# A streaming-encoder layer on one core: the order of side work in three late stages changed

## The chip, the cores and the metric

The kernel runs on one core of a Trainium2 chip. The metric is the device time of one execution, in microseconds (us). Three executions of the kernel before took 1586.19, 1580.94 and 1584.56 us; the median is 1584.56.

TensorE (PE, with PEld for its weight loads) multiplies matrices into PSUM, VectorE (DVE), ScalarE (ACT) and GpSimd (POOL) work elementwise, and SyncE (SP) issues nearly all transfers between the chip's memory and SBUF. Each engine runs its own instructions in order and waits for others by semaphores.

## The reference

One layer on x of 1024 frames by 1024 channels, all in 32-bit floats:

```python
for li in range(DEPTH):                                  # DEPTH = 1
    h = rmsnorm(x, norm_mix_g[li])
    z = h @ w_in[li]
    qa, fa, ia, ga, qb, kb, vb, gate_a, gate_b = jnp.split(z, split_at, axis=-1)
    oa = hgrn2_mixer(qa, fa, ia, ga, lower_bounds[li], hgrn_onorm_g[li])
    ob = band_attention(qb, kb, vb, ...)
    merged = (jax.nn.sigmoid(gate_a) * (oa @ w_branch_a[li])
              + jax.nn.sigmoid(gate_b) * (ob @ w_branch_b[li]))
    x = x + merged @ w_out[li]
    h2 = rmsnorm(x, norm_ffn_g[li])
    x = x + (jax.nn.silu(h2 @ w_ffn_gate[li]) * (h2 @ w_ffn_up[li])) @ w_ffn_down[li]
    h3 = rmsnorm(x, norm_ple_g[li])
    x = x + jax.nn.sigmoid(h3 @ w_ple_gate[li]) * (p[li] @ w_ple_proj[li])
return x
```

The feed-forward width is 2816, p has 256 columns.

## The kernel before, in words

**Layout.** The layer's x lies as eight tiles of 128 channels by 1024 frames. A matmul multiplies 128x128 weights by 128x512 operands into one PSUM bank of 128x512 (`pm`). To keep 32-bit accuracy, every operand is split into a high part, rounded by a cast on ScalarE, and a low rest, subtracted on VectorE or GpSimd; one product of two operands is three matmuls (`gemm`).

**Stages, in order of time.** The token mixers; 16 gate tiles, of which four are computed plainly and twelve in six Strassen units of two; the two branch products with their gates (`branches`, eight weight tiles); the output projection; the feed-forward gate and up products (22 Strassen units); the product down; and the last stage, `ple`, which computes the last line of the loop and stores the result.

**Products of seven passes.** The output projection, down and the last stage use the Strassen-Winograd scheme on 2x2 blocks: `passes` (L976) runs seven passes in the order of `KINDS` (L973): A11, S2, A12, S3, S1, A22, S4, each a weight block against an operand block B11, T2, B21, T3, T1, T4, B22. Three groups of four banks, x, y and z, accumulate chains of passes (`CHAIN`). In the last stage a pass has four steps (k) of four banks, 48 matmuls, and after a pass `after` (L1748) works on each of its four banks (u = 0 to 3). Its results are P1 (A11's), u2 and u3; `V.tensor_tensor(ps, ps, u2[u], ALU.add)` behind S1 adds u2 = P1+P6 into the banks of chain z, on which S4 then goes on. S4 runs bank by bank, the last bank in two halves of 256 frames (`last`, L1768).

**Finishing a tile of the last stage** (`out`, L1729) is a generator of four pieces: scaling by the rms row on VectorE (in place), a sigmoid on ScalarE, the product with the embedding e on VectorE (e<-t,e), and the addition of x, by GpSimd if nothing else is given, with the store issued by SP behind it (L1741). `todo` holds the tiles under way; `some(4)` moves four of them one piece on.

**Work beside the matmuls.** Each stage has a generator `side` of which one piece is issued after each step of the products; it holds sums for operands, loads, splits (`m_split`, L949: a cast on ScalarE and a subtraction s<-s,s of 128x1024 on VectorE) and the norm's rows. So the place of a `yield` sets where in an engine's order a piece stands.

**The order on the engines.** The instructions of V, A, G (VectorE, ScalarE, GpSimd through `Pinned`, L53), of TensorE (L82, L85) and of `load` and `store` (SP, L77) are chained by hand in the order in which the program issues them. The store in `out` is a plain `nc.sync.dma_start` outside that chain, which the scheduler places.

**Weights.** `weights` (L127) keeps a ring of four split tiles (`RING`) over two raw tiles (`RAW`): SP loads the raw tile (wr), ScalarE casts it (wh, L122), GpSimd subtracts the rest (wl, L125). `ahead` says how many tiles are prepared before they are used. In the Strassen units `strassen_weights` (L1389) makes sums of the next unit's weights on VectorE (q), casts them (whi) and takes the rest (wlo); `strassen_load` fetches the unit after that.

**Accumulating transfers.** Sums of weight blocks for the output projection and for down are made in the chip's memory: `dma_sums` (L1057) first copies blocks by SP and then adds others by DMAs that GpSimd issues (d<-in_wq and d<-d). Gate units, branches and feed-forward units take the additions one by one from the queue `self.adds` with `next(self.adds, None)` (L857, L909, L926, L1539); in a gate unit with every second piece of `side`, in a branch with each weight tile.

**Operands of the last stage.** `m_order` lists the operand tiles, two for each pass; `m_split` takes the next and puts it into `m_ready`, from which `operand` (L1778) takes. The first four splits are issued in down's last two passes (`down_side`, L1602), the rest in the last stage itself.

## Time and profile before

| what | us |
|---|---|
| three executions, median | 1584.56 |
| the profiled execution | 1583.47 |
| its span, from the first to the last instruction | 1581.7 |
| TensorE busy, of a mean granted clock of 0.997 | 1553.5 |
| busy in the span's last stretch, 1490 to 1582: TensorE | 79.99 |
| VectorE there | 62.99 |
| ScalarE there | 42.28 |
| GpSimd there | 42.75 |

The stretches by stage, with TensorE's (PE), its weight loads' (PEld), VectorE's, ScalarE's and GpSimd's busy time, each with its count of instructions, then the granted clock, the busy share of the DMA engines and their GB/s:

```profile
0.00:330.00 330.00, 320.60 (x2174) 285.28 (x2174) 195.10 (x384) 88.80 (x143) 93.56 (x53) 1.00 0.19 66
330.00:640.00 310.00, 306.96 (x1944) 261.30 (x1944) 236.67 (x597) 189.87 (x441) 79.64 (x49) 1.00 0.49 142
640.00:700.00 60.00, 58.63 (x255) 47.40 (x254) 27.92 (x30) 18.14 (x23) 22.34 (x14) 1.00 0.95 307
700.00:882.00 182.00, 181.69 (x815) 150.21 (x815) 147.67 (x156) 88.36 (x116) 69.32 (x36) 1.00 0.55 177
882.00:1252.00 370.00, 367.87 (x1616) 304.11 (x1615) 281.62 (x309) 104.64 (x156) 218.87 (x129) 1.00 0.38 114
1252.00:1490.00 238.00, 237.75 (x1050) 196.53 (x1049) 154.28 (x137) 106.64 (x125) 121.04 (x52) 1.00 0.67 244
```

Mixers and attention fill the first two rows and more; the branches begin at about 666 us, the feed-forward's first up unit runs near 886, down from about 1252 and the last stage from about 1490.

A row of the profile reads: start in us, duration, engine, line, operation, tile out<-in, size; in square brackets the time that the engine stood idle before, and whose work ended it. The span of a row on GpSimd is rough. A matmul row may stand for several.

### The profile page before, as it was taken

What the parts mean: (1) busy time and instruction counts of PE and PEld (TensorE: products, weight loads), DVE (VectorE), ACT (ScalarE), POOL (GpSimd) and SP (SyncE); (2) the same over time, 40 slices, a digit from 0 to 9 for tenths busy, and PEclk for the clock granted to TensorE, in tenths of its full rate; (3) what the DMA queues carried; (4) which work ended last, traced back from release to release, by engine and by line L of the source; (5) the groups of instructions that cost most, each with busy time, mean ns of one, the idle gap of its engine ahead of it and who ended that gap; (6) DMA issues with size and microseconds to landing.
All of it is one profiled execution on the core that took longest, in us unless ns stands there. A gap on an engine that the chain in (4) does not pass through costs nothing.

```text
span 1581.7 us, 21492 instructions
## 1 busy us (share of the span) xinstructions
PE 1553.5 (98%) x8224; PEld 1311.6 (83%) x8224; DVE 1106.2 (70%) x1685; ACT 638.7 (40%) x1059; POOL 647.5 (41%) x353
## 2 busy tenths in 40 slices
PE   8999999999999999999999999999999999999997
PEld 6998988888888888788888788888888888888886
DVE  5656765378777876644898777777777757755577
ACT  5321221167677633321467322322222244455462
POOL 3422221223113044337320555666665545545453
PEclk9999999999999999999999999999999999999999
DMA  5101100362433466897344334444433288775334
GB/s 189 54 28 41 41 28 28 105 196 80 141 114 127 153 153 174 225 320 239 107 157 171 132 113 127 132 129 127 121 117 109 85 303 323 278 275 180 124 110 173
DMA packets 83527, 230.38 MB, mean 146 GB/s; under 512 B 8928, under 2 KB 9568, under 8 KB 82912
## 3 DMA queue, kind: packets, MB, share of 16 engines
q1 hardware_dynamic: 76880, 213.26, 38.5%
q0 software_dynamic: 6400, 15.73, 6.2%
q8 instruction: 64, 1.05, 0.3%
q14 instruction: 39, 0.32, 0.1%
q10 hardware_dynamic: 144, 0.02, 0.0%
HBM read 179.43 MB, written 81.00 MB: 165 GB/s over the span
## 4 chain that ended last, share of the span: by engine, by line
PE 78%; DVE 9%; DMA 2%; POOL 2%; ACT 2%; issue 2%; SPq 0%; DVEq 0%; ACTq 0%; POOLq 0%
PE pm L82 76%; DVE s L53 6%; PE pm L85 3%; DVE m L53 1%; POOL wl L125 1%; DMA wr<-d 1%; ACT s L53 1%; DMA s<-d 1%; ACT wh L122 1%; POOL s L53 1%; DVE q L53 0%; DVE t L53 0%; DMA wr<-in_ba 0%; DMA wr<-in_dw 0%; DVE wl L125 0%
## 5 line engine op out<-in xcount | busy, mean ns | idle before, releaser
L82 PE MATMUL pm<-s,wh 128*128 128x512 f32 (+1 forms) x1712 | 532.7, 392 | 7.2 <-ACT wh L122 5.3
L82 PE MATMUL pm<-s,whi 128*128 128x512 f32 x1568 | 484.2, 390 | 2.4 <-DVE t L53 2.4
L125 POOL TENSOR_TENSOR wl<-wr,wh 128x1024 fp32r<-128x1024 f32 (+2 forms) x100 | 248.5, 2495 | 361.3 <-ACT wh L122 346.9
L82 PEld LDWEIGHTS pm<-s,wh 128*128 128x128 f32 x1712 | 319.8, 189 | 75.8 <-ACT wh L122 5.3
L82 PEld LDWEIGHTS pm<-s,whi 128*128 128x128 f32 x1568 | 294.8, 188 | 64.2 <-DVE t L53 3.2
L53 DVE TENSOR_TENSOR s<-s,s 128x512 f32<-128x512 f32 (+3 forms) x228 | 281.9, 1269 | 79.1 <-ACT s L53 41.5
L82 PE MATMUL pm<-s,wl 128*128 128x512 f32 (+1 forms) x856 | 333.8, 390 | 0.5 <-POOL wl L125 0.5
L82 PE MATMUL pm<-s,wlo 128*128 128x512 f32 x784 | 305.7, 390 | 0.0
L82 PE MATMUL pm<-wh,s 128*128 128x256 f32 (+1 forms) x896 | 237.6, 340 | 0.0
L122 ACT CAST wh<-wr 128x1024 fp32r<-128x1024 f32 (+2 forms) x114 | 115.0, 1010 | 277.3 <-PE pm L82 155.6
L82 PEld LDWEIGHTS pm<-s,wl 128*128 128x128 f32 x856 | 161.2, 188 | 34.3 <-POOL wl L125 1.4
L53 DVE TENSOR_TENSOR t<-pm,t 128x512 f32<-128x512 f32 x138 | 95.1, 689 | 126.1 <-PE pm L82 107.4
L82 PEld LDWEIGHTS pm<-s,wlo 128*128 128x128 f32 x784 | 147.6, 188 | 31.5 <-DVE wlo L53 0.6
L82 PEld LDWEIGHTS pm<-wh,s 128*128 128x128 f32 x896 | 154.4, 190 | 14.0
L53 POOL TENSOR_TENSOR wlo<-wr,whi 128x512 fp32r<-128x512 f32 (+1 forms) x53 | 113.7, 2154 | 91.7 <-PE pm L82 67.2
L82 PE MATMUL pm<-wl,s 128*128 128x256 f32 (+1 forms) x448 | 147.5, 329 | 0.8 <-POOL wl L125 0.8
L53 POOL TENSOR_TENSOR wlo<-q,whi 128x512 fp32r<-128x512 f32 x52 | 81.7, 1571 | 86.1 <-ACT whi L53 52.9
L53 ACT CAST s<-s 128x1024 fp32r<-128x1024 f32 (+1 forms) x94 | 90.1, 980 | 58.3 <-DVE s L53 34.7
L53 POOL TENSOR_TENSOR s<-t,rb 128x512 f32<-128x512 f32 x44 | 71.6, 1627 | 98.8 <-ACT t L53 98.8
L53 ACT CAST whi<-q 128x512 fp32r<-128x512 f32 (+1 forms) x81 | 61.4, 758 | 99.3 <-PE pm L82 94.6
L53 ACT ACTIVATE t<-s 128x512 f32<-128x512 f32 x44 | 27.8, 633 | 159.0 <-DVE s L53 155.0
L82 PEld LDWEIGHTS pm<-wl,s 128*128 128x128 f32 x448 | 85.4, 191 | 6.3 <-POOL wl L125 1.0
(144 smaller groups left out, 1798.9 us busy)
## 6 DMA issues: line engine op xcount, KB each, us to landing
s<-d SPq DMA_DIRECT2D x67, 512.0 KB, 5.9
d<-s SPq DMA_DIRECT2D x87, 256.0 KB, 2.3
wr<-d SPq DMA_DIRECT2D x36, 512.0 KB, 3.5
wr<-in_sg SPq DMA_DIRECT2D x22, 512.0 KB, 3.7
wr<-in_su SPq DMA_DIRECT2D x22, 512.0 KB, 4.1
s<-in_x SPq DMA_DIRECT2D x21, 512.0 KB, 7.8
d<-in_wq SPq DMA_DIRECT2D x20, 512.0 KB, 9.5
d<-s SPq DMA_DIRECT2D x18, 512.0 KB, 5.2
```

The source lines that it names most:

```text
L53: return lambda *a, **k: self.trunk.order(op(*a, **k), self.key)
L82: return self.order(self.nc.tensor.matmul(*a, **k))
L85: return self.order(self.nc.tensor.transpose(*a, **k))
L122: self.nc.scalar.copy(hi[:, c], raw[:, c])
L125: rest.tensor_tensor(lo[:, c], raw[:, c], f32(hi[:, c]), ALU.subtract)
```

## The change

Five things are changed, all in the order or the place of work; what is computed stays the same, and no matmul is added or removed.

1. The last two of the six gate units no longer take additions from `self.adds` (`n < units - 2`). Four accumulating DMAs less are issued there; the queue stays in order, so each later taker gets an addition four places earlier in the queue, and its last four are issued in the feed-forward units 18 to 21, which took none.
2. In the first up unit (n == 1) of `ff_pairs`, `side` yields once before it starts the sums of the next weights.
3. `warm`, a tile of one column, gets a silu in the second branch and a sigmoid before down's last pass, and nobody reads it.
4. B22's two splits move from the last stage into down's sixth pass (`m_early`).
5. In the last stage, S3's result is taken over with a subtraction of u2 on VectorE where ScalarE copied it. The addition of u2 into the banks of chain z moves from behind S1 into `side`, after two of S1's four steps; the accumulation group of a bank is closed there (`cut`). In `out`, x is added by VectorE for A12's tiles (GpSimd before), by GpSimd for S1's and S4's (VectorE before), except the last half bank's, which stays with VectorE; A22's stay with GpSimd. The store is chained into SP's order, and A12's come one piece later (`late`). `last` finishes all tiles under way before the last bank's.

```diff
...
@@ -853,7 +853,7 @@
                     self.strassen_load()
                 yield
                 for i, _ in enumerate(more):
-                    if i % 2:
+                    if i % 2 and n < units - 2:
                         next(self.adds, None)
                     yield
 
@@ -936,6 +936,8 @@
                     yield 2592
             if dd == 1:
                 self.branch_sums(0)
+            if dd == 1:
+                self.A.activation(self.warm, self.ones, AF.Silu)
             if dd == 2:
                 self.x, self.xd = [], [None] * KC
                 for c in range(KC):
@@ -973,8 +975,8 @@
     KINDS = (("A11", "B11"), ("S2", "T2"), ("A12", "B21"), ("S3", "T3"), ("S1", "T1"), ("A22", "T4"), ("S4", "B22"))
     CHAIN = {"A11": "x", "A12": "x", "S2": "y", "S3": "y", "A22": "y", "S1": "z", "S4": "z"}
 
-    def passes(self, npairs, operand, after, side, last=None):
-        banks = {}
+    def passes(self, npairs, operand, after, side, last=None, banks=None):
+        banks = {} if banks is None else banks
         for kind, b in self.KINDS:
             chain = self.CHAIN[kind]
             if last and kind == "S4":
@@ -1000,6 +1002,7 @@
             if fresh:
                 banks[chain] = [self.mm() for _ in range(4)]
             ps = banks[chain]
+            cut = 1 if last and kind == "S1" else npairs
             for k in range(npairs):
                 i, j = divmod(k, 2)
                 if j == 0:
@@ -1010,7 +1013,7 @@
                     c = slice(j * HALF + u * P, j * HALF + u * P + P)
                     drain(self.gemm(
                         ps[u], [(w[0][:, c], w[1][:, c], hi[:, s], lo[:, s])], first=fresh and k == 0,
-                        last=k == npairs - 1, **({} if fresh else {"skip_group_check": True})))
+                        last=k in (npairs - 1, cut), **({} if fresh and k <= cut else {"skip_group_check": True})))
                 next(side, None)
                 yield 0
             for u in range(4):
@@ -1528,6 +1531,8 @@
             def side():
                 more = self.strassen_weights() if n + 1 < units else self.down_first()
                 keep = self.keep_acts(n // 2 - 1) if n % 2 == 0 else iter(())
+                if n == 1:
+                    yield
                 next(more, None)
                 if n + 2 < units:
                     self.strassen_load()
@@ -1621,14 +1626,20 @@
                 self.ple_part("B22", (i - 35) // 2)
             yield
         drain(sums)
-        self.m_order = [(b, i) for _, b in self.KINDS for i in range(2)]
+        self.m_order = [("B22", i) for i in range(2)]
         self.m_ready = []
         for i in range(11):
             if i < 8 and i % 2 == 0:
                 self.ple_part("B11", i // 2)
-            if i in (4, 8):
+            if i in (1, 3):
                 self.m_split()
-            yield
+            if i == 3:
+                self.m_early, self.m_ready = self.m_ready, []
+                self.m_order = [(b, i) for _, b in self.KINDS[:6] for i in range(2)]
+            if i in (5, 8):
+                self.m_split()
+            yield
+        self.A.activation(self.warm, self.ones, AF.Sigmoid)
         for i in range(11):
             if i < 4:
                 self.ple_part("B12", i)
@@ -1716,7 +1727,7 @@
         nc, V, A, G = self.nc, self.V, self.A, self.G
         h0, h1 = slice(0, HALF), slice(HALF, T)
         p1, u2, u3 = [[t[:, h] for t in (self.slot(), self.slot()) for h in (h0, h1)] for _ in range(3)]
-        es = {}
+        es, banks = {}, {}
 
         def load(odd, h):
             tiles = [self.slot() for _ in range(2)]
@@ -1726,7 +1737,7 @@
 
         todo = []
 
-        def out(c, h, t, add=G, sp=None):
+        def out(c, h, t, add=V, sp=None, late=True):
 
             sp = sp or slice(0, HALF)
             t, e = t[:, sp], es[c, h.start][:, sp]
@@ -1738,7 +1749,9 @@
             V.tensor_tensor(e, t, e, ALU.mult)
             yield
             add.tensor_tensor(e, e, self.x[c][:, at], ALU.add)
-            nc.sync.dma_start(self.out[c][:, at], e)
+            if late:
+                yield
+            self.store(self.out[c][:, at], e)
 
         def some(n):
 
@@ -1755,20 +1768,21 @@
                 todo.append(out(2 * u, h1, ps))
                 next(todo[-1])
             elif kind == "S3":
-                A.copy(u3[u], ps)
+                V.tensor_tensor(u3[u], ps, u2[u], ALU.subtract)
             elif kind == "S1":
                 V.tensor_tensor(u3[u], ps, u3[u], ALU.add)
-                V.tensor_tensor(ps, ps, u2[u], ALU.add)
-                todo.append(out(2 * u + 1, h0, u3[u], V))
+                todo.append(out(2 * u + 1, h0, u3[u], G, late=False))
             elif kind == "A22":
-                todo.append(out(2 * u + 1, h1, ps))
+                todo.append(out(2 * u + 1, h1, ps, G, late=False))
                 next(todo[-1])
                 next(todo[-1])
 
         def last(u, ps, sp):
             for _ in range(max(0, min(2, len(todo) - u))):
                 drain(todo.pop(0))
-            stream = out(2 * u, h0, ps, V, sp)
+            while u == 3 and todo:
+                drain(todo.pop(0))
+            stream = out(2 * u, h0, ps, V if u == 3 and sp.start else G, sp, late=False)
             next(stream)
             next(stream)
             todo.append(stream)
@@ -1776,6 +1790,8 @@
                 drain(todo.pop(0))
 
         def operand(b, i):
+            if b == "B22":
+                return self.m_early.pop(0)
             got = self.m_ready.pop(0)
             if len(self.m_ready) < 2:
                 self.m_split()
@@ -1819,7 +1835,10 @@
             del todo[:]
 
             load(1, h1)
-            for i in range(4):
+            yield
+            for u, ps in enumerate(banks["z"]):
+                V.tensor_tensor(ps, ps, u2[u], ALU.add)
+            for i in range(3):
                 yield
             load(0, h0)
             for i in range(4):
@@ -1828,7 +1847,7 @@
                     del todo[:4]
                 yield
 
-        yield from self.passes(4, operand, after, side(), last)
+        yield from self.passes(4, operand, after, side(), last, banks)
         while todo:
             drain(todo.pop(0))
 
```

**GpSimd at the end of the gate units.** The rows are GpSimd's order from the last but one gate unit into the branches; wlo are rests of summed weights, wl of the branches' first weights (in_ba), d the sums in memory. Before:

```order
L53 TENSOR_TENSOR wlo_6529<-wr_6386,whi_6528 128x512
L53 DMA d_3462<-in_wq 256x1x512
L53 TENSOR_TENSOR wlo_6565<-wr_6388,whi_6564 128x1024
L53 TENSOR_TENSOR wlo_6588<-q_6546,whi_6587 128x512
L53 DMA d_3846<-in_wq 256x1x512
L53 TENSOR_TENSOR wlo_6647<-q_6627,whi_6646 128x512
L53 DMA d_3539<-in_wq 256x1x512
L125 TENSOR_TENSOR wl_6667<-wr_6669,wh_6668 128x1024
```

Changed:

```order
L53 TENSOR_TENSOR wlo_6529<-wr_6386,whi_6528 128x512
L53 TENSOR_TENSOR wlo_6565<-wr_6388,whi_6564 128x1024
L53 TENSOR_TENSOR wlo_6587<-q_6546,whi_6586 128x512
L53 TENSOR_TENSOR wlo_6645<-q_6625,whi_6644 128x512
L125 TENSOR_TENSOR wl_6665<-wr_6667,wh_6666 128x1024
L125 TENSOR_TENSOR wl_6671<-wr_6673,wh_6672 128x1024
L125 TENSOR_TENSOR wl_6677<-wr_6679,wh_6678 128x1024
L53 TENSOR_TENSOR wl_6821<-wr_6823,wh_6822 128x1024
```

The three additions d<-in_wq in this piece are gone from between the rests; the next one stands with the branches' later weights.

**VectorE at the first up unit.** The rows are VectorE's order at the seam; q are sums for the next unit's weights, t<-pm,t sums of a finished product's bank (pm) with an earlier one, s the gate tiles. Before:

```order
L53 TENSOR_TENSOR t_8490<-pm_8102,s_7985 128x512
L53 TENSOR_TENSOR s_8384<-t_8490,rb_8405 128x512
L53 TENSOR_TENSOR q_8521<-wr_8500,wr_8502 128x512
L53 TENSOR_TENSOR q_8521<-q_8521,wr_8500 128x512
L53 TENSOR_TENSOR t_8544<-pm_8505,t_8519 128x512
L53 TENSOR_TENSOR q_8546<-wr_8500 128x512
L53 TENSOR_TENSOR wlo_8549<-q_8521,whi_8548 128x1024
L53 TENSOR_TENSOR t_8579<-pm_8505,t_8519 128x512
```

Changed:

```order
L53 TENSOR_TENSOR t_8487<-pm_8099,s_7982 128x512
L53 TENSOR_TENSOR s_8381<-t_8487,rb_8402 128x512
L53 TENSOR_TENSOR t_8530<-pm_8502,t_8516 128x512
L53 TENSOR_TENSOR q_8532<-wr_8497,wr_8499 128x512
L53 TENSOR_TENSOR q_8532<-q_8532,wr_8497 128x512
L53 TENSOR_TENSOR q_8555<-wr_8497 128x512
L53 TENSOR_TENSOR t_8572<-pm_8502,t_8516 128x512
L53 TENSOR_TENSOR t_8572<-pm_8503,t_8572 128x512
L53 TENSOR_TENSOR s_8381<-t_8572,s_8381 128x512
L53 TENSOR_TENSOR wlo_8558<-q_8532,whi_8557 128x1024
```

The two q sums that stood ahead of t_8544<-pm_8505 stand behind the same sum, now t_8530<-pm_8502.

**SP and VectorE in the last stage.** The rows are SP's order from S1's last weights on; wr are raw weights (from d, the sums in memory, or in_gw), s<-d loads of e, out<-s the stores of A12's tiles. Before:

```order
L77 DMA wr_13494<-d_12457 128x1024
L77 DMA wr_13544<-in_gw 128x1024
L77 DMA wr_13598<-in_gw 128x1024
L1741 DMA out<-s_13348 128x512 x2
L1741 DMA out<-s_13349 128x512 x2
L77 DMA s_13614<-d_8072 128x512
L77 DMA s_13614<-d_8074 128x512
L77 DMA s_13615<-d_8076 128x512
L77 DMA s_13615<-d_8078 128x512
L77 DMA wr_13634<-d_12023 128x1024
```

Changed:

```order
L77 DMA wr_13504<-d_12458 128x1024
L77 DMA wr_13554<-in_gw 128x1024
L77 DMA out<-s_13358 128x512 x2
L77 DMA out<-s_13359 128x512 x2
L77 DMA wr_13604<-in_gw 128x1024
L77 DMA s_13620<-d_8069 128x512
L77 DMA s_13620<-d_8071 128x512
L77 DMA s_13621<-d_8073 128x512
L77 DMA s_13621<-d_8075 128x512
L77 DMA wr_13644<-d_12024 128x1024
```

The four stores (two rows of two) stand ahead of the third weight load in place of behind it.

**VectorE in the same place.** Rows of 128x1024 are splits; s_13204, s_13205 and s_13214, s_13215 are u3's tiles, s_13202, s_13203 and s_13212, s_13213 u2's; pm_13592 to pm_13595 and pm_13598 to pm_13601 are the banks of chain z, pm_13332 to pm_13335 those of S3. Before:

```order
L53 TENSOR_TENSOR s_13539<-s_12768,s_13538 128x1024
L53 TENSOR_TENSOR s_13569<-s_12847,s_13568 128x1024
L53 TENSOR_TENSOR s_13585<-s_12571,s_13584 128x1024
L53 TENSOR_TENSOR s_13204<-pm_13592,s_13204 128x512
L53 TENSOR_TENSOR pm_13592<-pm_13592,s_13202 128x512
L53 TENSOR_TENSOR s_13204<-pm_13593,s_13204 128x512
L53 TENSOR_TENSOR pm_13593<-pm_13593,s_13202 128x512
L53 TENSOR_TENSOR s_13205<-pm_13594,s_13205 128x512
L53 TENSOR_TENSOR pm_13594<-pm_13594,s_13203 128x512
L53 TENSOR_TENSOR s_13205<-pm_13595,s_13205 128x512
L53 TENSOR_TENSOR pm_13595<-pm_13595,s_13203 128x512
```

Changed:

```order
L53 TENSOR_TENSOR s_13575<-s_12856,s_13574 128x1024
L53 TENSOR_TENSOR s_13214<-pm_13332,s_13212 128x512
L53 TENSOR_TENSOR s_13214<-pm_13333,s_13212 128x512
L53 TENSOR_TENSOR s_13215<-pm_13334,s_13213 128x512
L53 TENSOR_TENSOR s_13215<-pm_13335,s_13213 128x512
L53 TENSOR_TENSOR pm_13598<-pm_13598,s_13212 128x512
L53 TENSOR_TENSOR pm_13599<-pm_13599,s_13212 128x512
L53 TENSOR_TENSOR pm_13600<-pm_13600,s_13213 128x512
L53 TENSOR_TENSOR pm_13601<-pm_13601,s_13213 128x512
L53 TENSOR_TENSOR s_13214<-pm_13598,s_13214 128x512
L53 TENSOR_TENSOR s_13214<-pm_13599,s_13214 128x512
```

Two of three splits are gone ahead of S1's results, the subtractions of S3's banks have come in, and the four additions into pm stand as a group ahead of those to u3, one by one behind each of them before.

4 lines of the change are left out of this document (2 added, 2 removed).

## The prediction

> **What bounds the kernel now.** I read the page's busy line first, then busy time by stretches, then the chain of waits.
>
> ```profile
> span 1581.7 us, 21492 instructions
> PE 1553.5 (98%) x8224; PEld 1311.6 (83%) x8224; DVE 1106.2 (70%) x1685; ACT 638.7 (40%) x1059; POOL 647.5 (41%) x353
> ...
> 1560.00:1571.00 11.00, 10.54 (x58) 9.02 (x56) 11.00 (x19) 2.91 (x5) 2.59 (x3) 1.00 0.29 111
> 1571.00:1582.00 11.00, 0.00 (x0) 0.00 (x0) 7.16 (x14) 1.90 (x4) 2.85 (x2) 0.71 0.46 175
> ```
>
> TensorE (first pair in a stretch) has work for 1553.5 of 1581.7 us, and no matmul is added or removed. What can be won is the 28.2 us in which it has none, and time at a lower clock. The biggest piece is the end: from 1571 on it does nothing, while VectorE (third pair) is full before that and still busy after. The chain of waits names the other places:
>
> ```profile
> 656.31 10.35 DMA s<-d
> 666.74 1.05 ACT s L191
> 667.82 1.24 DVE s L192
> 669.10 85.08 PE pm L82 x374
> ...
> 886.12 366.39 PE pm L82 x1608
> ...
> 1537.95 6.75 POOL s L53 x3
> 1547.07 6.36 DMA wr<-d
> ```
>
> The change touches three of its breaks: a load at the branch stage's start, VectorE at the seam of gate and up, and the last stage. I cost each.
>
> **Four additions moved.** These are accumulating DMAs issued by GpSimd; they leave the last two gate units for later stages.
>
> ```profile
> 656.20 1.07 POOL L53 DMA_DIRECT2D d<-in_wq  x1 [1.73 <-issue]
> ...
> q0 software_dynamic: 779, 1.50, 34.9%
> ...
> 660.00:670.00 10.00, 8.63 (x35) 5.99 (x34) 9.41 (x9) 5.13 (x7) 2.07 (x1) 1.00 1.05 312
> ...
> 666.12 0.40 PE L82 MATMUL pm<-s,wh 128*128 128x512 f32 x1
> 666.68 0.50 PE L82 MATMUL pm<-s,wh 128*128 128x512 f32 x1 [0.17 <-DVE s L192]
> ...
> 667.84 0.49 PE L82 MATMUL pm<-s,wh 128*128 128x512 f32 x1 [0.42 <-ACT s L191]
> 669.10 0.50 PE L82 MATMUL pm<-s,wh 128*128 128x512 f32 x1 [0.77 <-DVE s L192]
> ```
>
> Matmuls start 0.227 us apart where nothing is missing (85.08/374 in the chain). From 666.12 to 669.10 are four steps (one start, between the second and third row, is left out): 2.98 us where 0.91 would do, so 2.07 are lost. The last two rows wait for the fourth load, its cast and its remainder. That load took 10.35 us in a stretch whose DMA share is 1.05. The queue row is of 645 to 672: additions took 34.9% of 27 us for 1.50 MB, so one of 512 KB takes 3.1 us of all engines. Without the one issued at 656.20 the load lands near 663.6, its cast ends at 664.7 and its remainder at 665.9, before it is asked for. The first two steps lose a few tenths to other tiles, so I take 1.8; the bounds are 0 (the loads crowd each other) and 2.07. At their new places the four add 4x1.07 us to GpSimd and 3.1 us of DMA each to units where the chain shows TensorE unbroken for 366.39 us although most of them carry one already: nothing.
>
> **The seam.** In the first up unit the sums for later weights come one product later, so VectorE meets the sum that frees a bank (t<-pm,t) first.
>
> ```profile
> 882.00 1.78 DVE L53 TENSOR_TENSOR q<-wr,wr 128x512 f32<-128x512 f32 x1
> 883.82 1.64 DVE L53 TENSOR_TENSOR q<-q,wr 128x512 f32<-128x512 f32 x1
> 885.38 0.68 DVE L53 TENSOR_TENSOR t<-pm,t 128x512 f32<-128x512 f32 x1
> 885.98 1.16 DVE L53 TENSOR_TENSOR q<-wr 128x512 f32<-128x512 f32 x1
> ...
> 883.21 0.58 ACT L53 COPY t<-pm 128x512 f32<-128x512 f32 x1
> ...
> 883.60 0.39 PE L82 MATMUL pm<-s,wlo 128*128 128x512 f32 x1
> 886.12 1.13 PE L82 MATMUL pm<-s,whi 128*128 128x512 f32 x2 [2.13 <-DVE t L53]
> ...
> 889.61 0.42 PE L82 MATMUL pm<-s,wlo 128*128 128x512 f32 x1
> ...
> 886.00:890.00 4.00, 3.88 (x10) 3.07 (x11) 3.37 (x3) 1.48 (x2) 4.00 (x3) 0.57 0.00 0
> ```
>
> The sum needs ScalarE's copy, done at 883.79. With the two q sums behind it, it runs from 883.82 to 884.50 and TensorE goes on at 884.56 in place of 886.12: 1.56. The wait also cost speed: the granted clock behind it is 0.57, and the eight steps from 886.12 to 889.61 took 3.49 us where 8x0.227 is 1.82: 1.67. A wait of 0.7 is left; those of 0.42 and 0.77 above left the clock at 1.00. Together 3.2. [...] Late next: the q sums (1.78+1.64+1.16) end at 889.1, the next t (0.7) at 889.8, and the product that needs its bank starts two products of 12 steps later, 884.56+24x0.227=890.0. So the bounds are 0 (the wait comes back there, clock and all) and 4.0 (no wait left).
>
> Preloading the two activation tables removes a load from the way of a sigmoid and of a silu that both wait for VectorE longer: nothing.
>
> **The last stage.**
>
> ```profile
> 1522.71 3.41 DVE L53 TENSOR_TENSOR s<-s,s 128x1024 fp32r<-128x1024 f32 x1
> 1528.44 1.21 DVE L53 TENSOR_TENSOR s<-s,s 128x1024 fp32r<-128x1024 f32 x1
> 1533.58 2.47 DVE L53 TENSOR_TENSOR s<-pm,s 128x512 f32<-128x512 f32 x4
> 1558.72 6.61 DVE L53 TENSOR_TENSOR s<-s,s 128x1024 fp32r<-128x1024 f32 x9 [4.74 <-ACT s L53]
> 1565.26 2.48 DVE L53 TENSOR_TENSOR pm<-pm,rb 128x512 f32<-128x512 f32 x4
> 1578.34 0.43 DVE L53 TENSOR_TENSOR s<-s,s 128x256 f32<-128x256 f32 x1
> ...
> 1535.66 9.39 SPq L1741 DMA_DIRECT2D out<-s  x4
> ...
> 1553.53 2.12 ACT L122 CAST wh<-wr 128x1024 fp32r<-128x1024 f32 x2 [14.20 <-DMA wr<-d]
> ...
> 1554.66 4.78 POOL L125 TENSOR_TENSOR wl<-wr,wh 128x1024 fp32r<-128x1024 f32 x2 [7.62 <-ACT wh L122]
> 1568.41 5.44 POOL L53 TENSOR_TENSOR s<-s,s 128x512 f32<-128x512 f32 x4 [8.97 <-DVE s L53]
> ...
> 1543.03 0.61 PE L82 MATMUL pm<-s,wh 128*128 128x512 f32 x2
> 1570.27 0.28 PE L82 MATMUL pm<-s,wl 128*128 128x256 f32 x1
> ...
> wr<-d SPq DMA_DIRECT2D x36, 512.0 KB, 3.5
> ```
>
> Now: four stores hold SP from 1535.66, since each waits for a GpSimd addition (2.25 each by the chain's row); the last weights load at 1547.07, ScalarE stands 14.20 us for them, and VectorE goes on only at 1558.72, with a split of B22 and eight more ahead of A22's results. It reaches those at 1565.26 and is 8.2 us behind when TensorE ends at 1570.55; from its end (1578.77) to the span's are 2.92.
>
> Then: x for A12 is added by VectorE, two splits of 1.2 to 3.4 are gone, ten of its later additions go to GpSimd, and the last loads leave SP near 1542. It gains four subtractions (ScalarE's copies before), and its four additions P1+P6 now stand in the middle of S1, where TensorE waits for them. What that costs: the e products end at 1536.05 now (1533.58+2.47), and 2.2 earlier, 1533.9, if the split ahead of them takes 1.21 in place of 3.41 (ScalarE now casts T1 ahead of the weights). Behind them stand two splits (1.21 each), four x additions, four subtractions (2.48/4=0.62 each) and the first addition (0.7): 8.1. A split beside GpSimd takes up to 2.2 more. TensorE asks at 1543.03; the addition is ready from 1542.0 to 1546.4, so the wait is 0 to 3.4. I take the early start and one split held 1.9, 1543.9: a wait of 0.8. The other three follow at 0.68, TensorE's own pace. Behind the waiting matmul stand S1's second half, A22 and S4, so the wait goes to the end in full.
>
> Then the load of A22's second weights is behind the A12 stores, not ahead. It would leave SP near 1540 and is needed in mid A22, 1554; load, cast and remainder are 3.5+1.06+2.4 (the page's row on landing, 2.12/2, 4.78/2), so they end by 1547. No cost.
>
> At the end: S1 ends 24 steps behind its middle, 1543.9+5.4=1549.3, the additions to u3 0.7 later; scaling and e products take 8x0.62=5.0, held by one remainder (2.4) and some of GpSimd's additions: 1559 at the latest; A22's eight steps of 0.62 end by 1564; S4's first quarter comes 60 steps behind S1, 1562.9. So VectorE is within a step when TensorE ends at 1571.35. Behind that stand scaling, ScalarE's sigmoid, product and addition of the last half quarter, at 0.43 each, and 0.3 that I allow for the gaps between the engines: 1573.4, and with 2.92 the span ends at 1576.3: 5.4 gained. Bounds: 6.2 without the mid-pass wait; 1.5 with that wait at its longest plus 1.7 for the clock.
>
> **Sum:** 1.8+3.2+5.4=10.4. The profiled execution took 1583.47, so 1573.1; it is 1.1 under the median, 1584.56, from which it is 1574.2. I forecast 1573.5.
>
> **Rivals.**
> - *The seam's wait moves to the fifth product.* For it: 0.2 us to spare, and q sums stretched to 1.78 beside GpSimd. 3.2 lost: 1576.7. Chance 0.12.
> - *VectorE is late in mid S1.* For it: 3.41 for a split of 1.21. Against: only two remainders of GpSimd lie there. 3.4+1.7 in place of 0.8: 1577.8. Chance 0.12.
> - [...] Chance 0.05.
> - *The loads crowd each other, and both waits above come too:* 1582.8, no change. Chance 0.09.
> - *GpSimd becomes the bound* of the last stage. Twelve additions at 2.25 (6.75/3 in the chain, the pace beside VectorE) behind the last remainder, at 1559.4 as before, end at 1586.4; with 2.9 and the wait of 0.8 the span is 1590.1, less 5.0 from the other places 1585.1, 3.4 more than now: 1586.9 to 1588.0 by the two bases, 1587.4, slower. It decides from about 2.0 us for each. Against: 5.44 for four, 1.36 each, once VectorE works on PSUM. [...] Chance 0.06.
>
> The forecast keeps 0.56. A measurement of this kernel can tell about 0.3% (4.75 us) from no change, so faster means under 1579.8. Forecast and the first three rivals lie there, 0.85; a little goes for their spread: faster 0.83, within 0.1, slower 0.07. The range: 1573.5 less 1.6 (the three upper bounds) and 2.6 (half the spread of the runs), 1569.5; above, the second rival plus 2.6, 1580.5.
>
> **What would show it.** TensorE without breaks near 667 and a clock of 1.00 behind the seam; a break under 1 us in mid S1; ScalarE's 14.20 for wr<-d gone; at most 5 us from the last matmul to the last VectorE row and store. A clock under 1.00 after 1540, or a GpSimd row as the last one before the final store, would prove it wrong.

## The result, and the profile after

| | before | changed |
|---|---|---|
| median of six runs, us | 1583.92 | 1573.98 |
| lowest to highest | 1580.94 to 1586.19 | 1573.47 to 1576.64 |
| profiled execution | 1583.47 | 1574.29 |
| its span | 1581.7 | 1572.5 |
| from TensorE's last matmul to the span's end | 11.15 | 5.99 |

The ratio, taken over all runs, is 0.9942, with a 95% interval of 0.9929 to 0.9955: faster by 9.2 us of 1583.9, between 7.1 and 11.2 (the two medians alone lie 9.9 apart). The forecast was 1573.5.

The page of the changed kernel's profile, its span and busy times:

```profile
span 1572.5 us, 21502 instructions
PE 1551.8 (99%) x8224; PEld 1311.9 (83%) x8224; DVE 1108.8 (71%) x1685; ACT 636.2 (40%) x1057; POOL 646.9 (41%) x357
```

As many matmuls as before in 9.2 us less. The chain of waits of the changed kernel, its late links (start, duration, engine, tile):

```profile
858.22 633.04 PE pm L82 x2796
1491.80 33.47 PE pm L82 x159
1526.43 11.74 DVE s L53 x14
1538.92 27.61 PE pm L82 x132
```

The links over a load near 656, over VectorE at 884 and over GpSimd's additions and S4's load at 1538 to 1553 are gone. One new link stands at 1526: VectorE ahead of the middle of S1, as the change asked for. Laid side by side, matmul by matmul, the two executions drift apart at these places:

| place (time in the changed kernel) | gained, us | by |
|---|---|---|
| start, to 664 | -0.01 | 0.13 lost up to 36, won back later |
| branches, 665 to 667 | 2.50 | waits for the fourth load and its split |
| 831 | -0.56 | a wait for a rest of VectorE's, not there before |
| 859 to 862 | -1.58 | half clock, not there before |
| seam, 883 to 886 | 4.02 | wait 2.29 and half clock behind it |
| between these, 832 to 883 | -0.10 | small steps |
| down, 1264 | 0.54 | a wait of 0.41, and a small one behind it |
| middle of S1, 1539 | -0.71 | the wait that was forecast |
| S1 to TensorE's end | -0.08 | |
| TensorE's end to the span's end | 5.16 | VectorE no longer behind |
| sum | 9.18 | 1581.69-1572.51 by the spans |

The branch stage in the changed kernel's timeline of TensorE (start, duration, operation; x2 means two in one row):

```profile
665.83 0.62 PE L82 MATMUL pm<-s,wh 128*128 128x512 f32 x2
666.29 0.39 PE L82 MATMUL pm<-s,wl 128*128 128x512 f32 x1
666.51 0.62 PE L82 MATMUL pm<-s,wh 128*128 128x512 f32 x2
```

No bracket, no wait: pairs and singles follow at 0.227 us each, where three brackets stood before.

The seam, in the timeline of the engines that take part:

```profile
881.35 0.58 ACT L53 COPY t<-pm 128x512 f32<-128x512 f32 x1
...
881.96 0.69 DVE L53 TENSOR_TENSOR t<-pm,t 128x512 f32<-128x512 f32 x1 [1.74 <-ACT t L53]
...
882.56 0.68 DVE L53 TENSOR_TENSOR q<-wr,wr 128x512 f32<-128x512 f32 x1
...
883.35 0.39 PE L82 MATMUL pm<-s,wlo 128*128 128x512 f32 x1
...
883.57 0.61 PE L82 MATMUL pm<-s,whi 128*128 128x512 f32 x2
```

The sum t<-pm,t now waits for ScalarE's copy alone, ends at 882.65, and the matmul that needs the bank goes on at its own pace, 0.22 behind the one ahead. But TensorE came here late. Windows over the two executions (from:to, length, busy times by engine, then the granted clock, DMA share and GB/s), the changed kernel:

```profile
858.00:863.00 5.00, 4.78 (x14) 3.82 (x15) 4.93 (x6) 4.09 (x6) 2.58 (x1) 0.66 0.31 111
...
886.00:890.00 4.00, 4.00 (x20) 3.30 (x19) 3.86 (x4) 1.49 (x3) 4.00 (x3) 1.00 0.25 82
```

and the one before:

```profile
858.00:863.00 5.00, 4.74 (x30) 4.14 (x29) 4.27 (x5) 4.51 (x7) 2.58 (x1) 1.00 0.27 105
```

The same piece of work (sixteen matmuls of one column for the norm, a wait of 0.26 us, then products) was followed by a clock of 0.66 here and of 1.00 before. The half clock behind 886 is gone, but one has come in at 859, where nothing was changed. This became the question of the study.

The last stage, middle of S1, in the timelines of TensorE and of VectorE. A row that stands for several has the form of the first: the six at 1528.83 are a split, four additions of x and a split.

```profile
1537.99 0.39 PE L82 MATMUL pm<-s,wl 128*128 128x512 f32 x1
1538.92 0.70 PE L82 MATMUL pm<-s,wh 128*128 128x512 f32 x2 [0.55 <-DVE pm L53]
```

```profile
1528.83 6.95 DVE L53 TENSOR_TENSOR s<-s,s 128x1024 fp32r<-128x1024 f32 x6
1535.70 2.47 DVE L53 TENSOR_TENSOR s<-pm,s 128x512 f32<-128x512 f32 x4
1538.09 2.48 DVE L53 TENSOR_TENSOR pm<-pm,s 128x512 f32<-128x512 f32 x4
```

VectorE comes to P1+P6 at 1538.09, the first is ready at 1538.78, and TensorE, which would have gone on at 1538.21, waits 0.71. And the end, in the timeline of all engines:

```profile
1562.11 6.93 POOL L53 TENSOR_TENSOR s<-s,s 128x512 f32<-128x512 f32 x6
...
1566.24 0.28 PE L82 MATMUL pm<-s,wl 128*128 128x256 f32 x1
1566.56 0.43 DVE L53 TENSOR_TENSOR pm<-pm,rb 128x256 f32<-128x256 f32 x1 [0.83 <-PE pm L82]
1567.02 0.37 ACT L53 ACTIVATE pm<-pm 128x256 f32<-128x256 f32 x1 [2.02 <-DVE pm L53]
1567.42 0.42 DVE L53 TENSOR_TENSOR s<-pm,s 128x256 f32<-128x256 f32 x1 [0.43 <-ACT pm L53]
1567.88 0.43 DVE L53 TENSOR_TENSOR pm<-pm,rb 128x256 f32<-128x256 f32 x1
1568.35 0.37 ACT L53 ACTIVATE pm<-pm 128x256 f32<-128x256 f32 x1 [0.96 <-DVE pm L53]
1568.75 0.42 DVE L53 TENSOR_TENSOR s<-pm,s 128x256 f32<-128x256 f32 x1 [0.43 <-ACT pm L53]
1569.21 0.42 DVE L53 TENSOR_TENSOR s<-s,s 128x256 f32<-128x256 f32 x1
```

VectorE now waits for TensorE (0.83). It begins on the first half of the last bank only when TensorE has ended both halves, and on the second half only behind the first one's product: from TensorE's end at 1566.52 to VectorE's at 1569.63 are 3.11 us. GpSimd's six additions (1.16 each in the mean, the last of half size) end 0.6 us ahead of it. ScalarE's wait of 14.20 for wr<-d is 2.77 now, and no part of the chain.

### The profile page after: what moved, and what is told of

Its sections match the earlier page's. It is cut to its first block, busy times and chain, and to the rows that moved or that the text cites. A ratio compares the mean times of both kernels' runs of the same rounds, so it can differ in the third digit from the quotient of the medians.

```text
span 1572.5 us, 21502 instructions
## 1 busy us (share of the span) xinstructions
PE 1551.8 (99%) x8224; PEld 1311.9 (83%) x8224; DVE 1108.8 (71%) x1685; ACT 636.2 (40%) x1057; POOL 646.9 (41%) x357
## 4 chain that ended last, share of the span: by engine, by line
PE 85%; DVE 7%; ACT 1%; issue 1%; POOL 1%; DMA 1%; DVEq 0%; ACTq 0%; POOLq 0%
PE pm L82 82%; DVE s L53 5%; PE pm L85 3%; DVE m L53 1%; POOL wl L125 1%; ACT s L53 1%; ACT wh L122 0%; DVE wl L125 0%; DMA wr<-in_fm 0%; DMA wr<-d 0%; DMA wr<-in_pp 0%; POOL m L555 0%; ACT m L53 0%; DVE pm L53 0%; ACT m L367 0%
## 5 line engine op out<-in xcount | busy, mean ns | idle before, releaser
L125 POOL TENSOR_TENSOR wl<-wr,wh 128x1024 fp32r<-128x1024 f32 (+2 forms) x100 | 245.3, 2458 | 372.8 <-ACT wh L122 370.6
```

The source lines that it names most:

```text
L125: rest.tensor_tensor(lo[:, c], raw[:, c], f32(hi[:, c]), ALU.subtract)
```

## The experiments

All are measured against the kernel before on the same chip. "Above the changed kernel" is the difference of the ratios to the changed kernel's 0.9942, times 1583.9 us; with intervals of 0.0012 to 0.0017 on each side it is sure to some 2 us only, so the traces have to tell the smaller parts apart. For the last stage each trace gives a second, finer measure: from the matmul in its first pass at which the chain above begins a link (1491.80 here, 1496.61 before) to the span's end.

**1. The additions back in the gate units.**

```diff
-                    if i % 2 and n < units - 2:
+                    if i % 2:
```

> The changed kernel with the four additions back in the last two gate units; nothing else differs. If the forecast's first term is right, the three breaks of TensorE between 666.1 and 669.1 come back and the time is 1.8 to 2.4 us above the changed kernel's (2.07 were lost there before, 2.36 were won in the changed kernel's trace). If the gain came from elsewhere (loads only shifted), the breaks stay away or come back with no time, 0 to 0.5 us.

Median 1577.45, ratio 0.9958 (0.9943 to 0.9973): 2.5 us above. TensorE's timeline, and a window behind it:

```profile
666.14 0.50 PE L82 MATMUL pm<-s,wh 128*128 128x512 f32 x1 [0.28 <-DVE s L192]
...
668.09 0.50 PE L82 MATMUL pm<-s,wh 128*128 128x512 f32 x1 [1.22 <-ACT s L191]
669.35 0.50 PE L82 MATMUL pm<-s,wh 128*128 128x512 f32 x1 [0.76 <-DVE s L192]
```

```profile
669.50:673.00 3.50, 3.50 (x10) 2.67 (x11) 2.29 (x4) 2.36 (x3) 0.00 (x0) 0.55 1.01 378
```

The three breaks are back; matmul by matmul they cost 3.1 us against the changed kernel. Behind them, unlike before, stands a half clock, which costs 1.6 us. Later this trace has neither the wait at 831 nor the half clock at 859, but a wait of 0.74 at the seam, and 3.2 are left at the end.

**2. The seam as before.**

```diff
-                if n == 1:
-                    yield
```

> The changed kernel without the one product of delay in the first up unit. Forecast's reading: the wait for t<-pm,t comes back with 2.2 us and the half clock behind it with 1.7 to 2.0, so 3.9 to 4.2 us above the changed kernel in every run, mean clock 0.001 lower. Rival, the half clock does not hang on this wait: 2.2 us above the changed kernel's in the median, the trace shows the wait with a full clock behind it in some runs, and spans scatter by steps of 1.6 us in both kernels alike.

Median 1575.2, ratio 0.9946 (0.9930 to 0.9962): 0.6 us above, neither 3.9 nor 2.2. TensorE's timeline and a window of this kernel:

```profile
883.70 0.72 PE L82 MATMUL pm<-s,whi 128*128 128x512 f32 x2 [0.56 <-DVE t L53]
```

```profile
858.00:863.00 5.00, 5.00 (x16) 3.95 (x15) 4.93 (x6) 4.11 (x7) 2.26 (x1) 0.66 0.35 123
```

The half clock stands at 858 again, as in the changed kernel's trace, and the wait at the seam is 0.72 in place of 2.29. The two belong together: TensorE comes to the seam 1.6 us later by the half clock, VectorE does not, and the wait shrinks by as much.

**3. The last stage as before**, with B22's splits; additions, seam and preloads as changed.

```diff
-    def passes(self, npairs, operand, after, side, last=None, banks=None):
+    def passes(self, npairs, operand, after, side, last=None):
...
-                V.tensor_tensor(u3[u], ps, u2[u], ALU.subtract)
+                A.copy(u3[u], ps)
...
-        def out(c, h, t, add=V, sp=None, late=True):
+        def out(c, h, t, add=G, sp=None):
```

> The changed kernel with the last stage and B22's splits as before; additions, seam and the two preloads as changed. Forecast's reading: 5.2 us more behind TensorE's end (11.2 in place of 6.0), 0.7 less for the wait in mid S1 that falls away: 4.5 us above the changed kernel, 4.0 to 5.5 with the scatter. Rival, part of the last stage's gain came from the parts ahead of it (loads that arrive earlier): under 3.5 us.

Median 1578.86, ratio 0.9971 (0.9959 to 0.9982): 4.6 us above. In its trace no wait stands in S1, and from TensorE's end to the span's end are 10.90 us; from the marked matmul to the end 84.84 in place of 80.71. So the last stage's gain is its own.

**4. No preload of the activation tables.**

```diff
-            if dd == 1:
-                self.A.activation(self.warm, self.ones, AF.Silu)
...
-        self.A.activation(self.warm, self.ones, AF.Sigmoid)
```

> The changed kernel without the two activations that preload tables. Forecast's reading: nothing, within 0.4 us of the changed kernel. Rival: a table load (ScalarE's, at the first silu of the feed-forward or the first sigmoid of the last stage) stands in the way of VectorE: 1.0 to 1.5 us above.

Median 1574.74, ratio 0.9942 (0.9925 to 0.9958): no difference, though the interval alone would not exclude the rival's 1.0 to 1.5. The traces do: the two table loads, 1.28 us each, stand at 865.50 and 1516.85 here and at 668.70 and 1444.69 in the changed kernel, and TensorE has no wait beside any of them. This trace has no half clock at 859, and then the seam's wait is there:

```profile
881.79 0.73 PE L82 MATMUL pm<-s,whi 128*128 128x512 f32 x2 [0.59 <-DVE t L53]
```

0.75 us by the starts (881.79 less 880.82+0.227): the 0.7 that the forecast left there.

**5 to 7: parts of the last stage undone one at a time.** The engines that add x:

```diff
-        def out(c, h, t, add=V, sp=None, late=True):
+        def out(c, h, t, add=G, sp=None, late=True):
...
-                todo.append(out(2 * u + 1, h0, u3[u], G, late=False))
+                todo.append(out(2 * u + 1, h0, u3[u], V, late=False))
...
-            stream = out(2 * u, h0, ps, V if u == 3 and sp.start else G, sp, late=False)
+            stream = out(2 * u, h0, ps, V, sp, late=False)
```

> The changed kernel with x added as before: by GpSimd for A12's tiles, by VectorE for S1's and S4's; the stores stay in SP's order. VectorE loses four additions ahead of the middle of S1 (2.7 us, so the wait of 0.7 there goes) and gains eight behind it (5.2 us) of which 1.4 fit into its idle time before TensorE's end. Forecast's reading (VectorE's work at the end sets the tail): 0.5 to 2 us above the changed kernel, with VectorE's additions as the last rows. Rival, the hold of SP by A12's stores is what cost time before: the second weight load of A22 leaves SP only at 1540 and a break of TensorE appears in A22 or S4, 3 us or more above.

B22's splits:

```diff
-            if i in (1, 3):
-                self.m_split()
-            if i == 3:
-                self.m_early, self.m_ready = self.m_ready, []
-                self.m_order = [(b, i) for _, b in self.KINDS[:6] for i in range(2)]
...
-            if b == "B22":
-                return self.m_early.pop(0)
```

> The changed kernel with B22's two splits in the last stage again, by VectorE and ScalarE. Two splits of 1.2 to 3.4 us come back on VectorE. Forecast's reading: VectorE is that much later at A22's and S4's results, less its 1.4 us of idle time: 1 to 3.5 us above the changed kernel. Rival: the splits fall into VectorE's idle stretch in front of S1's end (1540.6 to 1542.6) and cost nothing, within 0.5 us.

The place of P1+P6:

```diff
-            cut = 1 if last and kind == "S1" else npairs
+            cut = npairs
...
-                V.tensor_tensor(u3[u], ps, u2[u], ALU.subtract)
+                A.copy(u3[u], ps)
...
                 V.tensor_tensor(u3[u], ps, u3[u], ALU.add)
+                V.tensor_tensor(ps, ps, u2[u], ALU.add)
...
-            for u, ps in enumerate(banks["z"]):
-                V.tensor_tensor(ps, ps, u2[u], ALU.add)
```

> The changed kernel with P1+P6 added into the banks behind S1 as before, and ScalarE's copies of S3 in place of VectorE's subtractions; the rest as changed. The wait of 0.7 us in mid S1 goes, and VectorE has four additions (2.8 us) more behind S1, of which 1.4 fit into its idle time. Forecast's reading: TensorE ends 0.7 us earlier, the tail is 1.4 us longer, 0.7 us above the changed kernel in sum. Rival, the last stage's gain rests on the place in mid S1: 3 us above.

| kernel | median | ratio | wait in mid S1 | TensorE's end to span's end | marked matmul to span's end |
|---|---|---|---|---|---|
| before | 1583.92 | 1 | none | 11.15 | 85.08 |
| changed | 1573.98 | 0.9942 | 0.71 | 5.99 | 80.71 |
| 5: x's engines back | 1574.62 | 0.9949 (0.9933 to 0.9964) | none | 8.30 | 82.24 |
| 6: B22 split late | 1577.52 | 0.9962 (0.9947 to 0.9977) | 1.87 | 8.12 | 84.03 |
| 7: P1+P6 behind S1 | 1575.13 | 0.9950 (0.9933 to 0.9967) | none | 7.34 | 81.26 |

By the last column B22's early splits are worth 3.3 us, the engines of x 1.5 and the place of P1+P6 0.55, of 4.4 together; they overlap, probably since VectorE's idle time is used once. Six traces with the last stage as changed (changed; 1, 2, 4, 10, 11) have 80.71 to 81.03 in that column, so the 0.55 is little more than the scatter. In the sixth and seventh traces GpSimd's last addition ends 0.6 us behind VectorE's last row (1572.50 and 1571.92, 1570.64 and 1570.05), so that GpSimd has a part in their tails. No break of TensorE came for weights held behind A12's stores in the fifth run. The sixth shows the price of one more split ahead of P1+P6: its timelines of TensorE and VectorE,

```profile
1540.14 0.70 PE L82 MATMUL pm<-s,wh 128*128 128x512 f32 x2 [1.71 <-DVE pm L53]
```

```profile
1528.89 8.10 DVE L53 TENSOR_TENSOR s<-s,s 128x1024 fp32r<-128x1024 f32 x7
```

Seven where the changed kernel had six: 8.10 less 6.95 is one split of 1.15 more ahead of P1+P6, and TensorE's wait there grew by as much, 1.87 in place of 0.71.

**8. P1+P6 one step later, the last scaling ahead of the product before it.**

```diff
-            cut = 1 if last and kind == "S1" else npairs
+            cut = 2 if last and kind == "S1" else npairs
...
             yield
+            yield
             for u, ps in enumerate(banks["z"]):
...
-            while u == 3 and todo:
+            while u == 3 and todo and not sp.start:
```

> The changed kernel with two more moves: P1+P6 goes into the banks after three of S1's four steps in place of two, and the last half bank is scaled ahead of the product of the half before it. By the trace of the changed kernel: the wait of 0.7 us in mid S1 goes, since the additions were ready 1 us after TensorE asked and are now asked for 2.7 us later; the last scaling starts at 1567.0 in place of 1567.9, so the tail is 0.85 us shorter. Together 1.5 us below the changed kernel. Rival: the end of the span is set by GpSimd's additions and the stores behind them, then only the 0.7 shows.

Median 1574.2, ratio 0.9945 (0.9929 to 0.9961). The wait in S1 is gone, but the tail is 6.40, not 5.1; marked matmul to end 80.33. VectorE's timeline shows why:

```profile
1565.35 0.43 DVE L53 TENSOR_TENSOR pm<-pm,rb 128x256 f32<-128x256 f32 x1 [0.43 <-ACT pm L53]
```

The second scaling stands earlier in the order and then waits for ScalarE's sigmoid on the first half of the same bank.

**9. Tiles of their own for the last two scalings.**

```diff
-            V.tensor_tensor(t, t, self.rb[:, at], ALU.mult)
+            d = t if into is None else into
+            V.tensor_tensor(d, t, self.rb[:, at], ALU.mult)
+            t = d
...
-            stream = out(2 * u, h0, ps, V if u == 3 and sp.start else G, sp, late=False)
+            stream = out(2 * u, h0, ps, V if u == 3 and sp.start else G, sp, late=False, into=self.slot()[:, :HALF // 2] if u == 3 else None)
```

> The kernel of the eighth run (P1+P6 one step later, the last scaling ahead of the product before it), and the last bank's two halves are scaled into tiles of their own in place of the shared bank. In the eighth run the second scaling waited 0.43 us for the first half's sigmoid, which works in place on the same bank; with tiles of their own that wait goes: TensorE's end to the span's end 5.5 in place of 6.4 us, and from the last stage's start to the span's end 86.6 us in place of 87.4. Rival: the end of the span hangs on the stores behind GpSimd's additions, then 6.0 or more stay.

Median 1574.12, ratio 0.9935 (0.9921 to 0.9948); tail 6.67, 0.3 longer than in the eighth. The wait for the sigmoid went, and VectorE's products, which now read two operands from SBUF, ran into GpSimd's additions:

```profile
1568.36 2.60 DVE L53 TENSOR_TENSOR s<-s,s 128x256 f32<-128x256 f32 x3
```

Three instructions of a size that takes 0.42 (row 1569.21 above) take 2.60: the first product 1.40 and the addition 0.83, both beside an addition of GpSimd's, and the second product, which falls between two of these, 0.41.

**10. Deliberate waits.** One sum of the weights is repeated in nine feed-forward units:

```diff
-        V.tensor_tensor(q[:, h1], r1[:, h1], r2[:, h1], ALU.add)
+        for _ in range(times):
+            V.tensor_tensor(q[:, h1], r1[:, h1], r2[:, h1], ALU.add)
```

> The changed kernel with one sum of the weights repeated 3 to 8 times in nine of the feed-forward units (VectorE's work only; what is computed is the same), so that TensorE waits there for VectorE by 0 to some 6 us. If a wait of about 2.3 us by itself halves the clock behind it, as the forecast read the row at 886, every wait of over 2 us is followed by seven or eight matmuls 0.43 us apart. [...]

One execution, 1581.93. Four of the units have a wait, 0.97, 1.71, 2.43 and 0.98 us by the starts of the matmuls; the other repeats bring none, probably since VectorE has slack there. The two longest in TensorE's timeline, and the window behind the longest:

```profile
1095.51 0.73 PE L83 MATMUL pm<-s,whi 128*128 128x512 f32 x2 [1.55 <-DVE t L54]
```

```profile
1136.16 0.74 PE L83 MATMUL pm<-s,whi 128*128 128x512 f32 x2 [2.27 <-DVE t L54]
```

```profile
1136.00:1140.00 4.00, 3.84 (x17) 3.15 (x18) 3.15 (x6) 1.54 (x2) 0.00 (x0) 1.00 0.01 4
```

A bracket of 2.27 leaves the clock at 1.00, where one of 2.13 before was followed by 0.57. Between these two the length of the wait doesn't decide; the last section sets beside them how much of the time ahead TensorE's matmuls filled. No wait above 2.43 us came about.

**11. The changed kernel again.**

> The changed kernel once more, for its scatter beside the ninth run: a median of 1573.5 to 1575, spans in steps of about 1.6 us, and a half clock behind the norm's small matmuls near 858 in about half of the traces. Where it comes the wait near 883 is 0 to 0.1 us, where it does not 0.75.

Median 1574.47, ratio 0.9942 (0.9930 to 0.9955). No half clock at 858 in its trace, and a wait of 0.71 at 883: both as expected. Its five spans are 1571.5, 1572.6, 1572.7, 1573.5 and 1575.6 at mean clocks of 1.000, 0.998, 0.998, 0.998 and 0.997. The longer ones have the lower clock, though the program is the same; steps of 1.6 us, as expected, are not to be seen in five spans.

**12. The last bank whole**, with P1+P6 one step later.

```diff
-                    cuts = (0, HALF) if u < 3 else (0, HALF // 2, HALF)
+                    cuts = (0, HALF)
...
-            cut = 1 if last and kind == "S1" else npairs
+            cut = 2 if last and kind == "S1" else npairs
...
-            stream = out(2 * u, h0, ps, V if u == 3 and sp.start else G, sp, late=False)
+            stream = out(2 * u, h0, ps, V if u == 3 else G, sp, late=False)
```

> The changed kernel with P1+P6 added after three of S1's four steps (as in the eighth run) and S4's last bank finished whole in place of two halves, x added by VectorE. In the traces so far VectorE began on the first half only when TensorE had ended both, 0.04 us behind its last matmul, so the halves bring no early start; whole, scaling, sigmoid, product and addition take 0.69, 0.58, 0.68 and 0.68 by the rows, with 0.15 of gaps 2.8 us where the halves took 3.11. So the tail is 5.7 in place of 6.0 us, the wait of 0.7 in mid S1 goes, and from the last stage's start to the span's end 86.8 us in place of 87.8; in the median some 1 us below the changed kernel, which the scatter may hide. Rival: GpSimd's backlog (its additions end 1.8 us behind TensorE) holds VectorE's last addition, 6.0 or more stay.

Median 1573.38, ratio 0.9929 (0.9917 to 0.9941). VectorE's timeline at the end:

```profile
1565.62 0.70 DVE L53 TENSOR_TENSOR pm<-pm,rb 128x512 f32<-128x512 f32 x1 [0.68 <-PE pm L82]
1566.97 0.69 DVE L53 TENSOR_TENSOR s<-pm,s 128x512 f32<-128x512 f32 x1 [0.65 <-ACT pm L53]
1567.70 0.69 DVE L53 TENSOR_TENSOR s<-s,s 128x512 f32<-128x512 f32 x1
```

From TensorE's end at 1565.59 to VectorE's at 1568.39 are 2.80 us, as worked out; the last store's landing takes 0.25 of that back, and the tail is 5.94. With the wait in S1 gone, marked matmul to end is 79.73, 1.0 below the changed kernel and the shortest of all. This is the fastest version measured; it beats the kernel before beyond doubt, and whether it beats the changed one in the median, the overlapping intervals don't tell.

## Why the prediction came out right, and where its steps did not

**Additions moved: right, a little too small.** Forecast 1.8 with a bound of 2.07; the trace shows 2.50, the first run 3.1 in its trace and 2.5 by its ratio. The term counted from 666.12 on, but the first break had begun one matmul earlier: between 665.5 and 666.1 another 0.4 were lost. At their new places the four cost nothing that shows: TensorE's link in the chain runs unbroken from 858 to 1491. Whether the wait at 831 is their doing is open: eight of the twelve traces with the additions moved have it, the two without (before; 1) don't. The rival of crowding loads falls.

**The seam: the wait was right, the clock was wrong.** The forecast had the wait shrink by 1.56 with 0.7 left. In runs without a half clock ahead of the seam it is 0.71 to 0.75 (1, 4, 11), against 2.29 before. The step that failed is "The wait also cost speed": 1.67 of the 3.2 were booked on it, as a loss that goes with the wait. In the execution before it did follow that wait (0.57 from 886 to 890), but a longer one in the tenth run left the clock full (1.00 from 1136 to 1140), and the norm's small matmuls were followed by the half clock in three traces (0.66 from 858 to 863: changed; 2, 10) and not in four others (1.00 there: before; 1, and from 857 to 862: 4, 11). So a half clock comes without the seam's wait too: 1.58 were lost at 859. The third chance in the forecast's sum, 0.05, rests on nothing that a run shows; what the runs showed in its place is this half clock. Whether the seam's wait had a part in the one behind it they don't settle; the last section gives what stood ahead of each. In the total a half clock at 859 shows by less than its 1.6, since the delay of TensorE takes as much off the seam's wait, as far as there is one. What the delay of one product saves is then 0.72 (with a half clock at 859, second run against the changed kernel) or 1.55 (without), plus what it takes off the chance of a half clock, which these runs don't size.

The half clocks at 886 (before) and at 859 (changed) last 3.41 us each, with matmuls 0.43 us apart in place of 0.227, and the pauses ahead of them were of 2.29 and of 0.26 us.

**The last stage: right, 1.0 too large.** Forecast 5.4; the traces give 4.4 (85.08 less 80.71), the third run 4.1 in its trace and 4.6 by its ratio. The wait in mid S1 was forecast at 0.8 and is 0.71. The working holds there: of the two splits ahead of P1+P6 one takes 3.41 and one 1.21, where one held by 1.9 was assumed; one split more, in the sixth run, makes the wait 1.87. The term that was mis-sized is the tail, 4.95 forecast and 5.99 found. "VectorE is within a step when TensorE ends" holds, but the 0.3 allowed "for the gaps between the engines" took the last bank's first half for done by then. It begins only with TensorE's end, and the second half stands behind it: 3.11 in place of 2.0. Why the first half waits for the second's matmuls no run isolates (the program issues both halves' matmuls before either scaling, in the two loops over `parts`); that it does, the changed trace shows, and that whole is no slower than halved, the twelfth. So of the signs that were named all came but one (5.99 from the last matmul to the span's end in place of at most 5), and neither of the two that would have proved it wrong: the clock is full until TensorE's end, and VectorE's row is the last.

**What was costed at nothing.** The preloads: no difference in the fourth run. A22's second weights behind A12's stores: no break of TensorE behind 1539.

**GpSimd as the bound: the rival fell, but not for the reason given.** The 2.0 us from which it "decides" is the pace that leaves no gain at all. By the prediction's own figures (1559.4, 0.8 and 2.92 against an end at 1576.3) twelve additions would have set the end from 1.1 us each, and the 1.36 that was held against the rival lies above that. They took 1.31 in the mean (6.32 for four, 9.43 for eight). What saved the term is that the last remainder (1548.11, 2.67) ended at 1550.78 in place of 1559.4, with the loads earlier; the additions began at 1552.62 and ended 0.6 ahead of VectorE's:

```profile
1552.62 6.32 POOL L53 TENSOR_TENSOR s<-s,s 128x512 f32<-128x512 f32 x4 [1.84 <-DVE s L53]
1559.61 9.43 POOL L53 TENSOR_TENSOR s<-s,s 128x512 f32<-128x512 f32 x8 [0.67 <-DVE s L53]
```

**The sum.** 10.4 forecast, 9.2 by the ratio: 0.7 more at the branch, 0.8 less at the seam and 859 together (4.02 less 1.58 in place of 3.2), 1.0 less in the last stage, and two small places that the forecast did not have. That the forecast lies within 0.5 us of the measured median is in part luck: the miss at the branch offsets most of that at the seam. A wait for a rest of VectorE's came at 831 (0.56) and one near 1269 went (0.54). Both are not the change's alone: of the changed kernel's two traces the second (eleventh run) has no wait at 831, and the second, third, sixth, eighth and tenth runs have one near 1264 again. What sets them stays open.

**Slips in the working**, none of which moves the forecast. The last stage's lower bound is 5.4 less 2.6 for the longer wait less 1.7, so 1.1 and not 1.5. The three upper bounds add 1.9 and not 1.6 (0.27, 0.8 and 0.8), so the range would begin at 1569.0. Eight of VectorE's later additions go to GpSimd, not ten.

## What to carry to other kernels

A wait that is removed is paid out only as far as the engine next in line can follow: here any delay of TensorE ahead of the seam was absorbed by the seam's wait, so undoing that part alone cost 0.6 us where 2.3 had been seen. Before a low clock is charged to the wait in front of it, look for the same wait with a full clock elsewhere in the trace or in another execution: here a bracket of 2.13 had 0.57 behind it and one of 2.27 had 1.00. At the end of a program, halving the last piece helps only if the next engine may begin on the first half; the rows show whether it does (here it began 0.04 us behind TensorE's end, and the halves took 3.11 us where the whole took 2.80).

## What was not expected of the hardware

The half clock comes and goes from execution to execution: behind the norm's small matmuls it followed in the traces of the changed kernel and of the second and tenth runs (0.66) and not in those of the kernel before and of the first, fourth and eleventh runs (1.00). Waits of 1.71, 1.87 (sixth run) and 2.43 us were followed by none, while three brackets of 0.28, 1.22 and 0.76 (first run) were. In the kernel before the granted clock is 0.50 from 886.24 to 889.65 and again from 1575.73, behind TensorE's end (1570.55), to the end of the span; in the changed kernel from 859.05 to 862.47 and from 1569.02, behind 1566.52, to the end. The stretches below are as long as the half clocks at 886 and 859 and are laid end to end from the clock's changes in the same trace. In the kernel before, the seam's wait of 2.29 lies whole in one stretch; in the tenth run the wait of 2.43 lies in two:

```profile
882.82:886.24 3.42, 1.29 (x7) 0.76 (x6) 3.39 (x4) 2.23 (x4) 3.42 (x3) 1.00 0.41 138
886.24:889.65 3.41, 3.41 (x9) 2.64 (x10) 3.13 (x2) 1.24 (x2) 3.41 (x3) 0.50 0.00 0
```

```profile
1131.61:1135.02 3.41, 2.28 (x11) 1.54 (x9) 3.24 (x6) 0.00 (x0) 0.00 (x0) 1.00 0.01 2
1135.02:1138.44 3.42, 2.28 (x10) 1.88 (x11) 3.42 (x5) 2.00 (x2) 0.00 (x0) 1.00 0.00 0
```

Busy time counts the norm's matmuls of one column in full (1.84 us for sixteen). Counted instead is the share of a stretch that matmuls fill at 0.227 us for 512 columns, in proportion to their columns:

| trace | stretch | share | clock in the next |
|---|---|---|---|
| before | 882.82 to 886.24, the wait of 2.29 | 0.33 | 0.50 |
| changed | 855.64 to 859.05, the norm's matmuls | 0.35 | 0.50 |
| 1 | 666.41 to 669.82, the waits at the branch | 0.24 | 0.50 |
| 6 | 1537.12 to 1540.54, the wait of 1.87 | 0.43 | 1.00 |
| 10 | 1131.61 to 1138.44, the wait of 2.43 | 0.62 and 0.62 | 1.00 |
| 11 | 856.88 to 860.30, the norm's matmuls | 0.48 | 1.00 |

In the rows of this table the length of the wait does not tell the half clocks from the full ones, and the share does: 0.24 to 0.35 ahead of 0.50, 0.43 to 0.62 ahead of 1.00. In the two traces of the kernel before and of the changed one, the stretches in front of the half clocks at 886 and 859 are the emptiest from 13 us on to the stretch in which TensorE ends; the next emptiest have 0.46 each (before, 36.32 to 39.73, and changed, 36.44 to 39.85), and 1.00 behind them. What sets the times of the clock's changes, and whether the share is what decides, these runs don't show.

The changed kernel's trace and the eleventh run's are of the same program. The first has the wait of 0.56 at 831 and the half clock at 859, the second has neither. Whether the one brings about the other is not shown. One half clock costs about 1.6 us (1.58 at 859), and spans of the same program spread by 4.1 us (eleventh run) with the mean clock falling from 1.000 to 0.997.

In the ninth run two operations of VectorE with both operands in SBUF, of a size that takes 0.42 in the changed kernel (row 1569.21), took 1.40 and 0.83 beside GpSimd's additions. The changed kernel's products, which read one operand from PSUM beside the same additions, took 0.42 each (rows 1567.42 and 1568.75).
